# Attention tables on VectorE and ScalarE instead of GpSimd, and the lambda product queued six steps later

## The chip, the core and the metric

The kernel runs on one core of a Trainium2 chip. The metric is the time of one execution on the device in microseconds. The core's engines each work through a queue of their own in order: TensorE (PE, matrix products), VectorE (DVE), ScalarE (ACT), GpSimd (POOL) and SyncE (SP, which here issues the weight loads). An instruction that waits holds up everything behind it on its engine.

## What is computed

Two blocks follow each other on 256 tokens of width 2048 in fp32. The first has dilated-window attention beside bidirectional retention; the second has a layer of differential attention and a layer of forgetting attention. Cut to what the change touches:

```python
# dilated attention: three patterns (window, dilation) share one score matrix
mask = |rel| <= radius and the key lies in the same residue class; bias = -slope * |rel| * dilation
# retention, both directions
decay = where(rel >= 0, exp(max(rel, 0) * log_gamma), 0)
# differential attention: causal mask and ALiBi bias
sc = where(dist >= 0, q @ k - slope * dist, NEG)
lam = exp(sum(lq1 * lk1)) - exp(sum(lq2 * lk2)) + lam_init
a = softmax(sc1) - lam * softmax(sc2)
# forgetting attention: causal mask as an additive NEG
```

Each of these masks and biases is a table that does not depend on the inputs: `dl` (negative distance, hugely negative where no pattern reaches) and `cn` (by how many patterns a key is reached) for the dilated heads, `rp` and `rm` (distance forward and backward, huge on the other side) for retention, `dist` and `tri` for the causal heads. They are made once, when the kernel runs.

## The kernel before, in words

All weights are streamed from HBM in tiles of 128x1024 fp32 (512 KB), each into one of seven `raw` buffers; a buffer is loaded again when its user is done with it. There are two uses. A **projection chunk** is first split for precise fp32 products: ACT casts the tile to `hi` (line 1643), DVE computes `lo` = raw - hi (line 1645), and PE multiplies both parts with the activation tile `hy` (line 145, the helper of all products). There are three buffers of `hi` and of `lo`, and the preparation runs two chunks ahead of PE. A **modulation tile** is multiplied by the conditioning vector and added to an accumulator on DVE alone (line 1623, `acc`). A plan sets how many modulation tiles go between the chunks; up to chunk 13 there is a little more than one to a chunk.

Chunks are counted here from 0. A feature-major chunk is 24 matmuls of 256 columns in eight groups of three (`hi`, `hi`, `lo`), a token-major one twelve of 512. In the first round each projection takes three chunks: 0 to 2 and 3 to 5 are feature-major, 6 to 8 token-major, 9 to 11 feature-major, 12 to 14 token-major. After the last chunk of a projection its four PSUM banks are evacuated by ACT (line 789). There are five such banks, so that the next projection can begin with the fifth.

Small work is written as generators. After each chunk the scheduler's `tick` advances every active generator to its next `yield`, and what they issue goes into the engines' queues at that place. `columns` (begun at chunk 4) transposes loaded vectors with PE, copies them with DVE (lines 489 and 490), makes some constants, and then the elementwise product `lampr` (line 500); PE sums that over the partitions with a product by `ones` (line 503, recorded as line 145), ACT takes the exponential `lame` (line 505), DVE the difference `lam` (line 507). `dilated_tables` runs at the same time, `retention_tables` behind the dilated heads, `causal_tables` behind the retention gates. In all three POOL makes an integer ramp (`iota`) and then does most of the arithmetic, with single operations on DVE: the line 397 for `dl`, the two bitwise ones of line 401. The activation tile of a chunk, where it is not there yet, is made by DVE, ACT, ACT, DVE (lines 642, 633, 635, 636).

Of the kernel before, what the change touches and what calls it, by code (L numbers as in the profile page):

```python
# [9 lines left out]
F32 = mybir.dt.float32  # L10
F32R = mybir.dt.float32r
I32 = mybir.dt.int32
AF = mybir.ActivationFunctionType
ALU = mybir.AluOpType
AX = mybir.AxisListType

P = 128
S = 256
# [3 lines left out]
NEG = -1e30  # L22
HUGE = 1e34
# [75 lines left out]
def two_block_kernel(ctx: ExitStack, tc: tile.TileContext, a: dict, out: bass.AP):  # L99
# [22 lines left out]
    def blk():  # L122
        assert pfree["blk"] > 0
        pfree["blk"] -= 1
        return blkp.tile([P, CW], F32, tag="blk", name=uid("blk"))

    def need_blk(n_):
        return ("wait", lambda: pfree["blk"] >= n_)
# [7 lines left out]
    def t_(shape, tag, bufs=2, dt=F32):  # L136
        return tmp.tile(shape, dt, tag=tag, name=uid(tag), bufs=bufs)

    def c_(shape, name, dt=F32):
        return cst.tile(shape, dt, tag=name, name=name)  # L140

    V, AC, PE, GP = nc.vector, nc.scalar, nc.tensor, nc.gpsimd

    def mm(o, l, r, start, stop):
        PE.matmul(o, l, r, start=start, stop=stop, skip_group_check=True)  # L145
# [131 lines left out]
    make_identity(nc, ident)  # L277
    ones = c_([P, P], "ones")
    GP.memset(ones, 1.0)
    rows = lambda ap: ap.rearrange("o (k p) -> (o k) p", p=P)  # L280
    rows1 = lambda ap: ap.rearrange("(k p) -> k p", p=P)
    xw = a["x"].rearrange("b (t p) d -> p (b t) d", p=P)
# [98 lines left out]
    lg = c_([P, 8], "lg")  # L381

    def dilated_tables():

        for _ in range(4):
            yield ("get", "s")
        yield need_blk(1)
        tab = blk()
        dl, cn = tab[:, 0:512], tab[:, 512:1024]
        iv = t_([P, 512], "s", 4, I32)  # L390
        i2 = t_([P, 512], "s", 4, I32)
        df = t_([P, 512], "s", 4)
        ng = t_([P, 512], "s", 4)
        GP.iota(iv.rearrange("p (a b) -> p a b", a=2), pattern=[[P, 2], [-1, S]], base=S, channel_multiplier=1)
        GP.tensor_copy(df, iv)
        GP.tensor_scalar(df, df, -float(S), None, op0=ALU.add)
        V.scalar_tensor_tensor(dl, df, -1.0, df, op0=ALU.mult, op1=ALU.min)
        GP.tensor_scalar(cn, dl, -64.0, None, op0=ALU.is_ge)
        yield
        for m in (3, 15):  # L400
            V.tensor_scalar(i2, iv, m, None, op0=ALU.bitwise_and)
            GP.tensor_copy(ng, i2)
            GP.tensor_scalar(ng, ng, 0.0, None, op0=ALU.is_equal)
            GP.tensor_tensor(cn, cn, ng, op=ALU.add)
            yield
        GP.tensor_scalar(ng, cn, 0.0, -HUGE, op0=ALU.is_equal, op1=ALU.mult)
        GP.tensor_tensor(dl, dl, ng, op=ALU.add)
        for _ in range(4):
            yield ("free", "s")
        tb["dl"], tb["cn"] = dl, cn  # L410
        ready.add("dl")

    def retention_tables():

        yield from logsig(lg, dec, *(t_([P, 8], "ls", 3) for _ in range(3)))
        V.tensor_scalar(lg, lg, -1e-30, None, op0=ALU.min)
        yield ("get", "s")
        yield ("get", "s")
        yield need_blk(1)
        tab = blk()  # L420
        rp, rm = tab[:, 0:512], tab[:, 512:1024]
        ri = t_([P, 512], "s", 4, I32)
        rf = t_([P, 512], "s", 4)
        GP.iota(ri.rearrange("p (a b) -> p a b", a=2), pattern=[[-P, 2], [1, S]], base=0, channel_multiplier=-1)
        GP.tensor_copy(rf, ri)
        GP.tensor_scalar(rp, rf, 0.0, HUGE, op0=ALU.is_lt, op1=ALU.mult)
        GP.tensor_tensor(rp, rp, rf, op=ALU.add)
        yield
        GP.tensor_scalar(rm, rf, 0.0, HUGE, op0=ALU.is_gt, op1=ALU.mult)
        GP.tensor_tensor(rm, rm, rf, op=ALU.subtract)  # L430
        yield
        yield ("free", "s")
        yield ("free", "s")
        tb["rp"], tb["rm"] = rp, rm
        ready.add("rt")

    def causal_tables():

        yield ("get", "s")
        dist, tri, idr = c_([P, 384], "cz_dist"), c_([P, 256], "cz_tri", F32R), c_([P, P], "cz_id", F32R)  # L440
        ci = t_([P, 384], "s", 4, I32)
        GP.iota(ci[:, 0:256], pattern=[[1, 256]], base=-P, channel_multiplier=-1)
        GP.iota(ci[:, 256:384], pattern=[[1, 128]], base=0, channel_multiplier=-1)
        GP.tensor_copy(dist, ci)
        neg = ci.bitcast(F32)
        GP.tensor_scalar(neg, dist, 0.0, -HUGE, op0=ALU.is_gt, op1=ALU.mult)
        GP.tensor_tensor(dist, dist, neg, op=ALU.add)
        yield
        AC.activation(tri, neg[:, 128:384], AF.Copy, scale=-NEG / HUGE)
        AC.copy(idr, ident)  # L450
        yield
        yield ("free", "s")
        tb["dist"], tb["tri"], tb["idr"] = dist, tri, idr
        ready.add("cz")
# [29 lines left out]
    def columns():  # L484
# [13 lines left out]
        V.tensor_scalar(subc, v3[:, 36:38], 1.0 - LAM_INIT, None, op0=ALU.mult)  # L498
        pr = c_([P, 2], "lampr")
        V.tensor_tensor(pr, v3[:, 32:36:2], v3[:, 33:36:2], op=ALU.mult)  # L500
        pt = yield ("get", "ps")
        mm(pt[:, 0:2], ones, pr, True, True)
        yield
# [1229 lines left out]
```

## Time and profile before

| | us |
|---|---|
| median of 3 runs | 1528.02 (1525.21 to 1530.26) |
| profiled execution | 1529.11 |
| span of the profile, first to last instruction | 1527.3 |
| PE busy | 1482.3 (97%) |
| DVE busy | 1267.4 (83%) |
| ACT busy | 821.7 (54%) |
| POOL busy | 49.5 (3%) |
| HBM read | 433.88 MB, 285 GB/s over the span |

A share of busy time is a mean over stages, so the stretches around the change are read one by one. A timeline row gives the start, the length, the engine and line, the tile written and the tiles read, and in brackets how long the engine idled before it and who ended that. Matmuls overlap, so that a PE row is longer than the distance to the next.

### The profile page before, as it was taken

Reading aid. Unit: us, or ns where it says so; the run is one execution under the profiler, and the core shown is the slowest. Engines: PE = TensorE matmul, PEld = TensorE weight load, DVE = VectorE, ACT = ScalarE, POOL = GpSimd, SP = SyncE. Lnnn points to the kernel's source line nnn. Section 1 sums busy time; section 2 is a strip of 40 time slices with the busy share of each in tenths; the row PEclk is TensorE's granted clock in tenths of the full one; section 3 lists DMA queues with packets and bytes.
Section 4 is the critical chain, followed back from the end, with each engine's and each line's share of the span. In section 5 each row is a group of like instructions: output and inputs, shape, how many; then the busy total and the mean of one; then the engine's idle time right before and its main releaser. Section 6 shows DMA issues by size and latency. Waiting matters only on the chain.

```text
span 1527.3 us, 26803 instructions
## 1 busy us (share of the span) xinstructions
PE 1482.3 (97%) x10152; PEld 1376.9 (90%) x10152; DVE 1267.4 (83%) x1839; ACT 821.7 (54%) x1533; POOL 49.5 (3%) x50
## 2 busy tenths in 40 slices
PE   6899999999999899999999999999999999999997
PEld 5889999989999799899998899978899999999896
DVE  5889989999988787987879989988887856667786
ACT  4474463645644657444555654456444876566631
POOL 3500000021000000000000000000000000000000
PEclk9999999999999999999999999999999999999998
DMA  9899978879699798999788889867999966778761
GB/s 325 291 351 335 351 268 320 314 255 331 212 313 329 249 372 282 356 325 322 254 302 280 293 298 323 272 218 253 312 354 329 328 248 196 245 259 282 258 210 56
DMA packets 180357, 437.75 MB, mean 287 GB/s; under 512 B 16352, under 2 KB 51314, under 8 KB 180228
## 3 DMA queue, kind: packets, MB, share of 16 engines
q1 hardware_dynamic: 179620, 435.89, 82.7%
q8 instruction: 79, 1.29, 0.3%
q14 instruction: 50, 0.41, 0.1%
q0 software_dynamic: 544, 0.14, 0.1%
q10 hardware_dynamic: 64, 0.02, 0.0%
HBM read 433.88 MB, written 2.11 MB: 285 GB/s over the span
## 4 chain that ended last, share of the span: by engine, by line
PE 77%; DVE 12%; DMA 5%; ACT 3%; issue 2%; SPq 0%; DVEq 0%; ACTq 0%
PE pa L145 71%; DVE lo L1645 4%; PE ps L145 4%; DVE acc L1623 3%; DMA w<-fdr 2%; DMA raw<-in_w_ada_dram 2%; ACT hi L1643 2%; PE ps L528 1%; DMA raw<-in_w_in_dram 1%; DMA raw<-in_a_w_in_dram 0%; DVE hy L636 0%; ACT blk L789 0%; ACT w L633 0%; PE ps L1172 0%; DVE xT L657 0%
## 5 line engine op out<-in xcount | busy, mean ns | idle before, releaser
L145 PE MATMUL pa<-hy,hi 128*128 128x256 f32 x4640 | 854.4, 286 | 9.5 <-ACT hy L632 2.7
L1643 ACT CAST hi<-raw 128x1024 fp32r<-128x1024 f32 x463 | 484.5, 1048 | 525.1 <-PE pa L145 443.1
L145 PEld LDWEIGHTS pa<-hy,hi 128*128 128x128 f32 x4640 | 726.4, 192 | 15.1 <-ACT hy L632 3.1
L1645 DVE TENSOR_TENSOR lo<-raw,hi 128x1024 fp32r<-128x1024 f32 x463 | 567.8, 1228 | 201.7 <-ACT hi L1643 200.2
L145 PE MATMUL pa<-hy,lo 128*128 128x256 f32 x2320 | 659.0, 284 | 1.9 <-DVE lo L1645 1.9
L145 PE MATMUL pa<-hi,hy 128*128 128x512 f32 (+1 forms) x1520 | 457.3, 379 | 3.1 <-ACT hy L632 2.3
L145 PEld LDWEIGHTS pa<-hy,lo 128*128 128x128 f32 x2320 | 445.6, 192 | 2.9 <-DVE lo L1645 2.6
L1623 DVE SCALAR_TENSOR_TENSOR acc<-raw,cact,acc 128x1024 f32<-128x1024 f32 (+2 forms) x343 | 423.2, 1237 | 8.9 <-DMA raw<-in_w_ada_dram 8.2
L145 PEld LDWEIGHTS pa<-hi,hy 128*128 128x128 f32 x1520 | 279.0, 189 | 56.7 <-ACT hy L632 3.1
L145 PE MATMUL pa<-lo,hy 128*128 128x512 f32 (+1 forms) x760 | 284.9, 375 | 2.2 <-DVE lo L1645 2.2
L145 PEld LDWEIGHTS pa<-lo,hy 128*128 128x128 f32 x760 | 144.2, 190 | 27.7 <-DVE lo L1645 3.2
L789 ACT ACTIVATE blk<-pa 128x512 f32<-128x512 f32 (+1 forms) x96 | 51.7, 577 | 11.3 <-PE pa L145 8.7
L536 ACT ACTIVATE jk<-ps 128x128 f32<-128x128 f32 x158 | 43.5, 276 | 8.8 <-PE ps L528 5.1
L793 DVE TENSOR_TENSOR blk<-pa,blk 128x512 f32<-128x512 f32 x60 | 37.4, 682 | 0.3 <-PE pa L145 0.3
L145 PE MATMUL ps<-blk,blk 128*128 128x256 f32 (+1 forms) x176 | 37.3, 342 | 0.0
L145 PEld LDWEIGHTS ps<-blk,blk 128*128 128x128 f32 x176 | 30.1, 190 | 3.4 <-DVE blk L793 0.2
L636 DVE TENSOR_TENSOR hy<-w,hy 128x256 fp32r<-128x256 f32 x64 | 27.2, 426 | 5.8 <-ACT w L633 4.9
L536 ACT ACTIVATION_READ_ACCUMULATOR jk<-ps 128x1 f32 x158 | 30.8, 195 | 0.0
L1608 POOL MEMSET acc<- 128x1024 f32 x2 | 1.9, 952 | 859.2 <-PE ps L528 859.2
L633 ACT ACTIVATE w<-xT,B,A 128x256 f32<-128x256 f32 x32 | 19.2, 601 | 11.3 <-DVE xT L663 11.3
L528 PE MATMUL ps<-ident,acc 128*128 128x128 f32 x160 | 24.6, 278 | 0.2 <-DVE acc L1623 0.2
L635 ACT CAST hy<-w 128x256 fp32r<-128x256 f32 x58 | 23.6, 407 | 1.8
(295 smaller groups left out, 818.7 us busy)
## 6 DMA issues: line engine op xcount, KB each, us to landing
raw<-in_w_mod_dram SPq DMA_DIRECT2D x192, 512.0 KB, 5.5
raw<-in_a_w_in_dram SPq DMA_DIRECT2D x128, 512.0 KB, 5.7
raw<-in_w_in_dram SPq DMA_DIRECT2D x112, 512.0 KB, 5.6
raw<-in_w_ada_dram SPq DMA_DIRECT2D x80, 512.0 KB, 5.4
raw<-in_kv_w_mod_dram SPq DMA_DIRECT2D x64, 512.0 KB, 6.2
raw<-in_kv_w_dram SPq DMA_DIRECT2D x64, 512.0 KB, 5.3
raw<-in_b_w_in_dram SPq DMA_DIRECT2D x64, 512.0 KB, 5.1
raw<-in_w_out_dram SPq DMA_DIRECT2D x32, 512.0 KB, 5.2
```

The lines of the kernel that those rows point to most:

```text
L145: PE.matmul(o, l, r, start=start, stop=stop, skip_group_check=True)
L528: PE.transpose(pt[:, j * P : (j + 1) * P], sl.acc[:, (q + j) * P : (q + j + 1) * P], ident)
L536: AC.activation(jk, pt[:, j * P : (j + 1) * P], AF.Copy, accum_out=r[:, q + j : q + j + 1])
L633: AC.activation(hf, t, AF.Identity, bias=bi, scale=sc)
L635: AC.copy(h[:, 0, :], hf)
L636: V.tensor_tensor(h[:, 1, :], hf, h[:, 0, :].bitcast(F32), op=ALU.subtract)
L789: AC.activation(dst, src, AF.Copy, scale=sc)
L793: V.tensor_tensor(dst, src, dst, op=ALU.add)
L1608: GP.memset(sl.acc, 0.0)
L1623: V.scalar_tensor_tensor(ac, tn, c, ac, op0=ALU.mult, op1=ALU.add)
L1643: AC.copy(hi, t)
L1645: V.tensor_tensor(lo, t, hi.bitcast(F32), op=ALU.subtract)
```

## The change

The tables come to the same values in another way. POOL keeps the `iota`s and gets one more constant, `mS`. The steps behind them go to DVE (mostly operations that fuse two steps) and to ACT (conversions from integer, and `Relu(1 - x)` in place of a comparison with zero), one per scheduler step. `rm` now has the other sign, for which `lg[:, 4:8]` is negated. In `columns` six bare `yield`s go between `lampr` and the product that uses it.

```diff
--- before.py
+++ after.py
@@ -277,6 +277,8 @@
     make_identity(nc, ident)
     ones = c_([P, P], "ones")
     GP.memset(ones, 1.0)
+    mS = c_([P, 1], "mS")
+    GP.memset(mS, -float(S))
     rows = lambda ap: ap.rearrange("o (k p) -> (o k) p", p=P)
     rows1 = lambda ap: ap.rearrange("(k p) -> k p", p=P)
     xw = a["x"].rearrange("b (t p) d -> p (b t) d", p=P)
@@ -392,19 +394,26 @@
         df = t_([P, 512], "s", 4)
         ng = t_([P, 512], "s", 4)
         GP.iota(iv.rearrange("p (a b) -> p a b", a=2), pattern=[[P, 2], [-1, S]], base=S, channel_multiplier=1)
-        GP.tensor_copy(df, iv)
-        GP.tensor_scalar(df, df, -float(S), None, op0=ALU.add)
+        yield
+        yield
+        V.tensor_scalar(i2, iv, 3, None, op0=ALU.bitwise_and)
+        yield
+        AC.activation(df, iv, AF.Identity, bias=mS)
+        AC.activation(ng, i2, AF.Relu, bias=ones[:, 0:1], scale=-1.0)
+        yield
         V.scalar_tensor_tensor(dl, df, -1.0, df, op0=ALU.mult, op1=ALU.min)
-        GP.tensor_scalar(cn, dl, -64.0, None, op0=ALU.is_ge)
-        yield
-        for m in (3, 15):
-            V.tensor_scalar(i2, iv, m, None, op0=ALU.bitwise_and)
-            GP.tensor_copy(ng, i2)
-            GP.tensor_scalar(ng, ng, 0.0, None, op0=ALU.is_equal)
-            GP.tensor_tensor(cn, cn, ng, op=ALU.add)
-            yield
-        GP.tensor_scalar(ng, cn, 0.0, -HUGE, op0=ALU.is_equal, op1=ALU.mult)
-        GP.tensor_tensor(dl, dl, ng, op=ALU.add)
+        yield
+        V.scalar_tensor_tensor(cn, dl, -64.0, ng, op0=ALU.is_ge, op1=ALU.add)
+        yield
+        V.tensor_scalar(i2, iv, 15, None, op0=ALU.bitwise_and)
+        yield
+        AC.activation(ng, i2, AF.Relu, bias=ones[:, 0:1], scale=-1.0)
+        yield
+        V.tensor_tensor(cn, cn, ng, op=ALU.add)
+        yield
+        AC.activation(ng, cn, AF.Relu, bias=ones[:, 0:1], scale=-1.0)
+        yield
+        V.scalar_tensor_tensor(dl, ng, -HUGE, dl, op0=ALU.mult, op1=ALU.add)
         for _ in range(4):
             yield ("free", "s")
         tb["dl"], tb["cn"] = dl, cn
@@ -414,6 +423,7 @@
 
         yield from logsig(lg, dec, *(t_([P, 8], "ls", 3) for _ in range(3)))
         V.tensor_scalar(lg, lg, -1e-30, None, op0=ALU.min)
+        V.tensor_scalar(lg[:, 4:8], lg[:, 4:8], -1.0, None, op0=ALU.mult)
         yield ("get", "s")
         yield ("get", "s")
         yield need_blk(1)
@@ -422,12 +432,12 @@
         ri = t_([P, 512], "s", 4, I32)
         rf = t_([P, 512], "s", 4)
         GP.iota(ri.rearrange("p (a b) -> p a b", a=2), pattern=[[-P, 2], [1, S]], base=0, channel_multiplier=-1)
-        GP.tensor_copy(rf, ri)
-        GP.tensor_scalar(rp, rf, 0.0, HUGE, op0=ALU.is_lt, op1=ALU.mult)
-        GP.tensor_tensor(rp, rp, rf, op=ALU.add)
-        yield
-        GP.tensor_scalar(rm, rf, 0.0, HUGE, op0=ALU.is_gt, op1=ALU.mult)
-        GP.tensor_tensor(rm, rm, rf, op=ALU.subtract)
+        yield
+        AC.copy(rf, ri)
+        yield
+        V.scalar_tensor_tensor(rp, rf, -HUGE, rf, op0=ALU.mult, op1=ALU.max)
+        yield
+        V.scalar_tensor_tensor(rm, rf, -HUGE, rf, op0=ALU.mult, op1=ALU.min)
         yield
         yield ("free", "s")
         yield ("free", "s")
@@ -441,13 +451,12 @@
         ci = t_([P, 384], "s", 4, I32)
         GP.iota(ci[:, 0:256], pattern=[[1, 256]], base=-P, channel_multiplier=-1)
         GP.iota(ci[:, 256:384], pattern=[[1, 128]], base=0, channel_multiplier=-1)
-        GP.tensor_copy(dist, ci)
-        neg = ci.bitcast(F32)
-        GP.tensor_scalar(neg, dist, 0.0, -HUGE, op0=ALU.is_gt, op1=ALU.mult)
-        GP.tensor_tensor(dist, dist, neg, op=ALU.add)
-        yield
-        AC.activation(tri, neg[:, 128:384], AF.Copy, scale=-NEG / HUGE)
+        yield
+        AC.copy(dist, ci)
         AC.copy(idr, ident)
+        yield
+        V.tensor_scalar(tri, dist[:, 128:384], NEG, 0.0, op0=ALU.mult, op1=ALU.min)
+        V.scalar_tensor_tensor(dist, dist, -HUGE, dist, op0=ALU.mult, op1=ALU.min)
         yield
         yield ("free", "s")
         tb["dist"], tb["tri"], tb["idr"] = dist, tri, idr
@@ -498,6 +507,8 @@
         V.tensor_scalar(subc, v3[:, 36:38], 1.0 - LAM_INIT, None, op0=ALU.mult)
         pr = c_([P, 2], "lampr")
         V.tensor_tensor(pr, v3[:, 32:36:2], v3[:, 33:36:2], op=ALU.mult)
+        for _ in range(6):
+            yield
         pt = yield ("get", "ps")
         mm(pt[:, 0:2], ones, pr, True, True)
         yield
```

What stands where now is shown at three places. Names are tile names with a buffer number; behind the change a line of the kernel has a number higher by 2 to 11.

PE, at the lambda product (`ps<-lampr,ones`; `hi88` and `lo89` belong to chunk 4, `hi94` and `lo95` to chunk 5). Before:

```order
L145 MATMUL pa100_529<-hy58_347,hi88_473 128x256 x2
L145 MATMUL pa100_529<-hy58_347,lo89_474 128x256
L145 MATMUL ps106_600<-lampr_598,ones_85 128x2
L145 MATMUL pa97_526<-hy83_431,hi94_520 128x256 x2
L145 MATMUL pa97_526<-hy83_431,lo95_521 128x256
```

Now (`hi126` and `lo127` belong to chunk 10, `hi133` and `lo134` to chunk 11):

```order
L145 MATMUL pa139_732<-hy58_349,hi126_686 128x256 x2
L145 MATMUL pa139_732<-hy58_349,lo127_687 128x256
L145 MATMUL ps144_794<-lampr_589,ones_85 128x2
L145 MATMUL pa136_729<-hy83_429,hi133_723 128x256 x2
L145 MATMUL pa136_729<-hy83_429,lo134_724 128x256
```

The product has moved from between chunks 4 and 5 to between chunks 10 and 11; nothing else on PE has moved.

DVE, from chunk 2 to the tables' first operations (`lo68` is chunk 2's, `lo81` chunk 3's, `lo89` chunk 4's, `lo95` chunk 5's, `lo104` chunk 6's; `blk74` holds `dl` and `cn`, `hy83` is an activation tile). Before:

```order
L1645 TENSOR_TENSOR lo68_380<-raw45_308,hi67_379 128x1024
L397 SCALAR_TENSOR_TENSOR blk74_413<-s77_416 128x512
L1623 SCALAR_TENSOR_TENSOR acc51_332<-raw50_330,cact_92,acc51_332 128x1024
L642 TENSOR_TENSOR w182_429<-xT_95,rst_97 128x256
L1645 TENSOR_TENSOR lo81_427<-raw52_334,hi80_426 128x1024
L636 TENSOR_TENSOR hy83_431<-w184_432,hy83_431 128x256
L401 TENSOR_SCALAR s76_415<-s75_414 128x512
...
L1645 TENSOR_TENSOR lo89_474<-raw63_359,hi88_473 128x1024
L401 TENSOR_SCALAR s76_415<-s75_414 128x512
```

Now, from the last of the column constants, which stand behind chunk 6's split as before, to chunk 9 (`lo108` is chunk 7's, `lo115` chunk 8's, `lo123` chunk 9's):

```order
L509 TENSOR_TENSOR lampr_589<-v3_92 128x2
L404 SCALAR_TENSOR_TENSOR blk74_415<-s77_418 128x512
L1634 SCALAR_TENSOR_TENSOR acc51_334<-raw86_462,cact_94,acc51_334 128x1024
L1656 TENSOR_TENSOR lo108_596<-raw87_465,hi107_595 128x1024
L406 SCALAR_TENSOR_TENSOR blk74_415<-blk74_415,s78_419 128x512
L1634 SCALAR_TENSOR_TENSOR acc51_334<-raw90_471,cact_94,acc51_334 128x1024
L1634 SCALAR_TENSOR_TENSOR acc51_334<-raw93_509,cact_94,acc51_334 128x1024
L1656 TENSOR_TENSOR lo115_639<-raw96_515,hi114_638 128x1024
L408 TENSOR_SCALAR s76_417<-s75_416 128x512
L1634 SCALAR_TENSOR_TENSOR acc51_334<-raw102_551,cact_94,acc51_334 128x1024
L1656 TENSOR_TENSOR lo123_665<-raw105_557,hi122_664 128x1024
```

The first table operation has moved from behind chunk 2's split to behind `lampr`; the rest are spread up to chunk 13's split, and one bitwise operation stays behind chunk 4's. `lam`, which stood behind chunk 7's split, now stands behind chunk 13's.

ACT, around the table operations (`hi94` is chunk 5's, `hi103` chunk 6's, `hi133` chunk 11's, `hi141` and `hi145` those of 12 and 13). Now:

```order
L1654 CAST hi94_511<-raw69_385 128x1024
L401 ACTIVATE s77_418<-s75_416,mS_87 128x512
L402 ACTIVATE s78_419<-s76_417,ones_85 128x512
L1654 CAST hi103_553<-raw85_435 128x1024
...
L1654 CAST hi133_723<-raw116_642 128x1024
L414 ACTIVATE s78_419<-blk74_415,ones_85 128x512
L1654 CAST hi141_764<-raw124_668 128x1024
L1654 CAST hi145_797<-raw125_684 128x1024
L800 ACTIVATE blk148_830<-pa136_729 128x512
...
L516 ACTIVATE lame_836<-ps144_794 128x2
```

The activations are new in this queue; `lame` has moved from behind the evacuation of chunks 3 to 5 to behind that of chunks 9 to 11.

## Rows read from the trace of the kernel before

**Rows 1.** the page, part 1: busy us, share of the span, instructions of each engine

```profile
PE 1482.3 (97%) x10152; PEld 1376.9 (90%) x10152; DVE 1267.4 (83%) x1839; ACT 821.7 (54%) x1533; POOL 49.5 (3%) x50
```

**Rows 2.** waits of PE, whole run: us in total, times, longest us

```profile
PE ps L145 <- DVE lampr L500: 4.5, 1, 4.5
```

**Rows 3.** timeline of PE: start, length in us, what, [idle before, releaser]

```profile
45.17 0.38 PE L145 MATMUL pa<-hy,hi 128*128 128x256 f32 x1 [0.52 <-ACT hy L635]
...
59.42 0.56 PE L145 MATMUL ps<-lampr,ones 128*128 128x2 f32 x2 [4.50 <-DVE lampr L500]
59.84 0.77 PE L145 MATMUL pa<-hy,hi 128*128 128x256 f32 x2
...
65.11 0.56 PE L145 MATMUL pa<-hi,hy 128*128 128x512 f32 x1
...
79.21 0.40 PE L145 MATMUL pa<-hy,hi 128*128 128x256 f32 x2
...
82.09 0.40 PE L145 MATMUL pa<-hi,hy 128*128 128x512 f32 x1
```

**Rows 4.** stretch of chunk 5: us, busy us of each engine, granted clock, DMA share, GB/s

```profile
59.40:65.10 5.70, 5.68 (x26) 5.70 (x27) 2.21 (x2) 1.79 (x3) 3.27 (x2) 0.50 0.84 285
```

**Rows 5.** timeline of DVE, 41 to 73 us

```profile
41.77 0.68 DVE L397 SCALAR_TENSOR_TENSOR blk<-s 128x512 f32<-128x512 f32 x1
...
45.79 0.41 DVE L401 TENSOR_SCALAR s<-s 128x512 int32<-128x512 int32 x1
...
50.42 1.55 DVE L401 TENSOR_SCALAR s<-s 128x512 int32<-128x512 int32 x1
...
56.19 2.30 DVE L1645 TENSOR_TENSOR lo<-raw,hi 128x1024 fp32r<-128x1024 f32 x1
...
59.13 0.15 DVE L500 TENSOR_TENSOR lampr<-v 128x2 f32<-128x2 f32 x1
...
66.04 0.16 DVE L507 TENSOR_TENSOR lam<-lame 128x1 f32<-128x1 f32 x1 [4.43 <-ACT lame L505]
...
71.15 1.22 DVE L1645 TENSOR_TENSOR lo<-raw,hi 128x1024 fp32r<-128x1024 f32 x1
72.29 1.28 DVE L1623 SCALAR_TENSOR_TENSOR acc<-raw,cact,acc 128x1024 f32<-128x1024 f32 x1
```

**Rows 6.** timeline of POOL, the last operation but one of the dilated tables

```profile
57.50 2.79 POOL L406 TENSOR_SCALAR s<-blk 128x512 f32<-128x512 f32 x1
```

**Rows 7.** stretches: columns as in Rows 4 (PE, PEld, DVE, ACT, POOL)

```profile
25.00:50.00 25.00, 18.68 (x104) 16.75 (x105) 21.31 (x31) 12.73 (x29) 7.37 (x3) 1.00 1.01 372
50.00:70.00 20.00, 15.50 (x89) 14.50 (x88) 15.49 (x21) 7.12 (x10) 11.90 (x7) 0.83 0.71 244
...
75.00:110.00 35.00, 34.60 (x221) 30.95 (x219) 30.01 (x45) 24.28 (x50) 0.00 (x0) 1.00 1.01 352
110.00:140.00 30.00, 29.21 (x240) 28.74 (x239) 29.00 (x36) 14.88 (x20) 0.00 (x0) 1.00 0.91 325
```

**Rows 8.** timeline of ACT, three casts of chunks

```profile
75.85 1.05 ACT L1643 CAST hi<-raw 128x1024 fp32r<-128x1024 f32 x1 [1.59 <-DMA raw<-in_w_in_dram]
...
143.47 1.06 ACT L1643 CAST hi<-raw 128x1024 fp32r<-128x1024 f32 x1 [2.85 <-DMA raw<-in_w_in_dram]
...
165.53 1.05 ACT L1643 CAST hi<-raw 128x1024 fp32r<-128x1024 f32 x1 [1.83 <-PE pa L145]
```

**Rows 9.** chain of waits back from 130 us: start, length, what

```profile
31.93 7.33 DMA raw<-in_w_ada_dram
```

**Rows 10.** the page, part 5: busy us, mean ns of one, idle before

```profile
L789 ACT ACTIVATE blk<-pa 128x512 f32<-128x512 f32 (+1 forms) x96 | 51.7, 577 | 11.3 <-PE pa L145 8.7
```

**Rows 11.** timeline of DVE, a split beside the retention tables

```profile
327.93 2.31 DVE L1645 TENSOR_TENSOR lo<-raw,hi 128x1024 fp32r<-128x1024 f32 x1
```

**Rows 12.** timeline of PE behind that split

```profile
330.30 0.50 PE L145 MATMUL pa<-lo,hy 128*128 128x512 f32 x1 [0.56 <-DVE lo L1645]
```

**Rows 13.** stretch of the causal tables, columns as in Rows 7

```profile
370.00:385.00 15.00, 15.00 (x79) 13.01 (x78) 14.66 (x16) 9.12 (x22) 5.76 (x5) 1.00 0.71 240
```

## The prediction, made before the changed kernel was run

> **What bounds the kernel now.** I read the page first, then the list of waits, then the stretches in which something waits. TensorE (PE) is busy for 97% of the span [rows 1], so a microsecond counts only where PE stands still or runs at a lower clock. The longest single wait of PE after its start is 4.5 us, for the product that gives lambda (`lampr`) [rows 2].
>
> The timeline of PE shows the place [rows 3]. PE idles 4.50 us, the product begins at 59.42, chunk 5 at 59.84. Chunk 5 then runs at half the rate: its 24 matmuls take 59.84 to 65.11 = 5.27 us, where the like ones of chunk 11 take 79.21 to 82.09 = 2.88. The granted clock was 0.50 in that stretch [rows 4], which is 1.2 of 2.4 GHz, after 4.5 us in which PE had idled.
>
> Why `lampr` is late is in the timeline of VectorE (DVE) [rows 5]: it comes at 59.13, behind the split of chunk 6 (`lo`, 56.19), which takes 2.30 us where 1.22 is usual (71.15). The bitwise table operation at 50.42 takes 1.55, the same one 0.41 at 45.79. These two alone cost 2.2 us. GpSimd (POOL) works on the tables beside them, 2.79 us for one operation [rows 6]. DVE afterwards idles 4.43 us more for `lam` [rows 5], which needs an exponential on ScalarE (ACT) that stands behind the evacuation of chunk 5.
>
> A stalled DVE frees no raw buffers, so transfers stop: 372 GB/s in 25 to 50, 244 in 50 to 70, then 352 in 75 to 110 [rows 7]. The loads are close behind PE here: ACT waits for a transfer at 75.85 and still at 143.47; at 165.53 it waits for PE [rows 8]. So what PE gains before 80 us must be fed by transfers up to some 145, and is then kept to the end, since the order of every engine is unchanged beyond the tables and lambda.
>
> **The change, part by part.** The sum is made against the profiled execution, 1529.1 us, which is 1.1 above the median of 1528.0.
>
> *Lambda product six steps later.* It goes from behind chunk 4 to behind chunk 10. Its operand is made behind the split of chunk 6, so at chunk 10 it has long been there: -4.5 us. The product's own 0.42 (59.42 to 59.84) moves along; I count nothing for it. With no idling ahead of it chunk 5 runs like chunk 11: 2.88 - 5.27 = -2.4 us.
>
> *POOL's eleven operations on the dilated tables.* Chunk 2 waits 0.52 us for its activation tile (45.17) [rows 3]. Ahead of that tile in DVE's order stands the first table operation (41.77, 0.68) [rows 5], which now comes some four chunks later. Between 0 and -0.5; I take -0.5, since more than that leaves the queue. PE's demand is thus 7.4 us earlier from chunk 6 on.
>
> *Six operations on DVE instead of three.* DVE's operations follow each other about 0.08 sooner than their length (71.15 + 1.22 against 72.29) [rows 5]. Two bitwise ones at 0.33 and four of 0.60 come to 3.1 us, against 1.3 for the three of before without stretching. Is DVE in time? From 39.3, when the tile of an accumulation has just landed (31.93 + 7.33) [rows 9], to the split of chunk 11 the new order has 13 accumulations at 1.19 (15.5, from 72.29), ten splits at 1.14 (11.4), five table operations (2.5), the column constants (0.8, from the end of 56.19 to that of 59.13) and two operations of 256 elements for one activation tile (0.7, an estimate from the 0.68 of 512): 30.9 us, so 70.2 without a wait. PE began chunk 11 at 79.21 and will want it at 71.8. It fits by 1.6: cost 0, as long as the transfers keep up.
>
> *Do they?* Behind the tile of 39.3 up to chunk 11's own 21 must land: twelve for accumulations, nine for chunks 3 to 11, of 524,288 bytes, 11.0 MB. At 372 GB/s that is 29.6 us, so 68.9; with 1.05 for the cast `hi` [rows 8] and 1.22 for `lo` the chunk is ready at 71.2, in time. At the 352 of 75 to 110 it is 31.3 us, ready at 72.9, 1.1 late. At the 325 of 110 to 140 it is 33.8 us and 3.6 late [rows 7]. So this step gives back between 0 and 3.6; I take +1.1, since 75 to 110 is the nearest stretch in which the loads were catching up.
>
> *ACT.* Four activations of 128x512 at about 0.58 [rows 10] are put between its casts: two behind the cast of chunk 5, one behind that of chunk 9, one behind that of chunk 11. Their operands come from DVE operations that stand ahead of those casts' splits, so I expect no waiting. The cast of chunk 6 comes up to 1.2 us later; its split ends by 55.7 (58.5 now, less 2.2 and 0.6), and PE wants it at 57.7. Cost 0; wholly uncovered, the four would be 2.3. The two later tables add three small copies or casts to an engine busy for 54% [rows 1], less one activation: 0.
>
> The Trainium skill's page "ScalarE: Activation LUTs", section "Rules for kernel authors", speaks against this part: relu, max, add and the like belong on VectorE, not on ScalarE. By its figures (section "What ACT_TABLE_LOAD costs": 280 ns and 0.833 ns an element with a pointer bias) an activation of 512 would take 0.71 us, an estimate. The row's 0.58 is lower, and decides. By the page the sum would lose up to 2.8 us, if nothing covered the four.
>
> *Retention tables, 308 to 330.* POOL's chain stretches DVE here too: the split at 327.93 takes 2.31 us instead of 1.22 [rows 11], and PE waits 0.56 for it at 330.30 [rows 12]. That 1.1 goes, and two operations of 0.60 and a tiny one come to DVE, one of them behind this split: -0.5 (0 to -0.56).
>
> *Causal tables, near 375.* DVE gets two operations. PE is busy for all of 370 to 385 [rows 13] and has two chunks ready ahead of it: 0. POOL's new memset of one column, 0.1 us ahead of its first DMAs, delays nothing that PE waits for: 0.
>
> Sum: -4.5 - 2.4 - 0.5 + 1.1 - 0.5 = **-6.8 us**. The profiled execution would take 1522.3, the median 1521.2.
>
> **The rivals.**
> - *The loads do not follow.* The hole of 50 to 70 is not filled, since raw buffers still come free too slowly with DVE full for 30.9 of 32.5 us. With the 244 GB/s of before [rows 7] chunk 11 would be ready at 86.7, later than now: no gain is left. Between that and the 3.6 of the part above lie 1524 to 1528, say 1525.5. Against it: 25 to 50 ran at 372 with DVE busy for 21.3 of 25 us. Chance 0.17.
> - *All of it* (faster still). The transfers run at 372 and nothing is given back: -4.5 - 2.4 - 0.5 - 0.56 = -8.0, and up to 1 us more where loads came late behind the hole (the wait at 75.85): 1519.5 or less. Against it: DVE itself then has 1.6 us to spare and no more. Chance 0.14.
> - *ACT's detour costs* (the rule above as a mechanism). The casts of chunks 6, 10 and 12 come up to 2.3 us late in all and nothing covers it: -4.5, so 1523.5. For it: splits and matmuls meet closely under the new demand. Against: ACT idles 1.83 us before a cast when all is in time (165.53). Chance 0.05.
> - *The wait returns as `lam` on DVE* (slower). `lam` now stands behind the split of chunk 13, and its exponential on ACT behind the evacuation of chunks 9 to 11, thus behind PE. If DVE gets there two chunks ahead of PE, it waits 5.8 us and four evacuations, 2.4: 8.2. Nothing frees a buffer meanwhile, and a new transfer takes 7.3 to land [rows 9]; PE has the two chunks, 5.8, so it idles 9.7 and then runs at half the clock for some two chunks, 4.8. Less the 7.9 gained that is +6.6: 1534.6. From a wait of 6.3 us on it is slower by 0.3%. Against: by the counts above DVE is not before 74.5 at `lam`, and PE ends chunk 11 at 74.7, with some 0.8 of evacuation and exponential behind it: a wait of about 1 us. Chance 0.05.
> - *The product waits again* (no change). That needs `lampr` to come later than chunk 10 in DVE's time, while it stands behind the split of chunk 6, four chunks earlier. Chance 0.01.
>
> **How the numbers follow.** The forecast has the remaining 0.58. About 0.3% (4.6 us) is what a measurement of this kernel can tell from no change, so faster means below 1523.4. The forecast, but for its edge where 3.6 is given back, and the larger gain lie there, with a little of the ACT case: 0.73. Same: the loads' case, that edge, the rest of ACT's: 0.22. Slower: 0.05. The range of 1517 to 1526 takes in the larger gain, with the scatter of the runs below it, and most of the loads' case.
>
> **What would show it.** Right: no PE wait on `lampr`; granted clock 1.00 from 45 to 90; splits of 1.2 us in 45 to 62; chunk 11 beginning near 72; 350 GB/s or more in 50 to 70; POOL with little but iotas and memsets; no wait at 330. Wrong: PE waits for `lo`, or ACT for transfers, for more than 3 us together in 60 to 90, or DVE waits for `lam` over 4 us again.

## The result, and the profile after

The changed kernel takes 1518.14 us (median, 1517.29 to 1520.17), the kernel before 1527.74 in the same session: ratio 0.9935, 95% interval 0.9917 to 0.9953, that is 9.6 us less. It was measured once more, in another session, at 1520.62 against 1527.63: ratio 0.9955, 0.9940 to 0.9971, 7.0 us less. The profiled execution took 1518.92 us, with a span of 1517.1. Two of the executions timed below ran far longer than the rest, one of the later product alone (5111.66 us) and one of POOL's work without its use (1678.05); the ratios leave them out, and without them the two medians would be 1525.14 and 1527.11.

The page, part 1, of the changed kernel [rows 1]:

```profile
PE 1479.0 (97%) x10152; PEld 1375.5 (91%) x10152; DVE 1262.9 (83%) x1847; ACT 824.3 (54%) x1538; POOL 13.2 (1%) x32
```

The shares of PE, DVE and ACT are those of before; POOL alone shows the change. The waits say more. Waits of PE in the changed kernel, whole run (us in total, times, longest), the first, the fifth and the sixth:

```profile
PE ps L299 <- DMA s<-in_c_dram: 5.5, 1, 5.5
...
PE pa L145 <- ACT blk L800: 3.4, 1, 3.4
PE pa L145 <- DVE lo L1656: 2.7, 3, 1.6
```

The row for `lampr` [rows 2] is gone, and in 38 to 100 us, where before had waits of 4.5, 0.5 and 0.4 us, this view is empty. The timeline of PE shows the same places as [rows 3]:

```profile
44.49 0.66 PE L145 MATMUL pa<-hy,hi 128*128 128x256 f32 x2
...
53.59 0.40 PE L145 MATMUL pa<-hy,hi 128*128 128x256 f32 x2
...
56.47 0.40 PE L145 MATMUL pa<-hi,hy 128*128 128x512 f32 x1
...
70.41 0.28 PE L145 MATMUL ps<-lampr,ones 128*128 128x2 f32 x2
70.54 0.48 PE L145 MATMUL pa<-hy,hi 128*128 128x256 f32 x2
70.86 0.28 PE L145 MATMUL pa<-hy,lo 128*128 128x256 f32 x1
```

Chunk 2 begins at 44.49 without a wait. Chunk 5 runs from 53.59 to 56.47 = 2.88 us instead of 5.27. The lambda product at 70.41 waits for nothing and is 0.13 ahead of chunk 11 at 70.54 (79.21 before, 71.8 forecast). Stretches of the changed kernel, columns as in [rows 7]:

```profile
25.00:50.00 25.00, 19.54 (x113) 17.96 (x113) 21.39 (x30) 13.67 (x31) 0.00 (x0) 1.00 1.02 372
50.00:70.00 20.00, 20.00 (x137) 18.57 (x136) 19.93 (x26) 12.36 (x18) 0.00 (x0) 1.00 1.04 392
```

In 50 to 70 us the clock is 1.00 where it was 0.83, PE and DVE are busy throughout, and the loads move 392 GB/s where they moved 244. The timeline of DVE shows why [rows 5, 11]:

```profile
44.28 0.43 DVE L647 TENSOR_TENSOR hy<-w,hy 128x256 fp32r<-128x256 f32 x1
...
52.14 1.22 DVE L1656 TENSOR_TENSOR lo<-raw,hi 128x1024 fp32r<-128x1024 f32 x1
...
53.97 0.15 DVE L509 TENSOR_TENSOR lampr<-v 128x2 f32<-128x2 f32 x1
54.05 0.68 DVE L404 SCALAR_TENSOR_TENSOR blk<-s 128x512 f32<-128x512 f32 x1
...
69.34 1.22 DVE L1656 TENSOR_TENSOR lo<-raw,hi 128x1024 fp32r<-128x1024 f32 x1
70.48 1.28 DVE L1634 SCALAR_TENSOR_TENSOR acc<-raw,cact,acc 128x1024 f32<-128x1024 f32 x1
...
74.57 0.16 DVE L518 TENSOR_TENSOR lam<-lame 128x1 f32<-128x1 f32 x1
...
320.63 1.22 DVE L1656 TENSOR_TENSOR lo<-raw,hi 128x1024 fp32r<-128x1024 f32 x1
```

Chunk 6's split (52.14) and those of the retention stage (320.63) take 1.22 us again, `lampr` comes at 53.97 instead of 59.13, and `lam` (74.57) has no wait. Chunk 11's split ends at 70.56; PE begins that chunk at 70.54 and first reads `lo` at 70.86. DVE's last operation on the activation tile of chunk 2 (44.28) takes 0.43 us; before, with POOL at work, it took 0.72:

```profile
45.15 0.72 DVE L636 TENSOR_TENSOR hy<-w,hy 128x256 fp32r<-128x256 f32 x1
```

On ACT, two of the new activations and two casts behind them:

```profile
49.31 0.73 ACT L401 ACTIVATE s<-s,mS 128x512 f32<-128x512 int32 x1
49.93 0.71 ACT L402 ACTIVATE s<-s,ones 128x512 f32<-128x512 int32 x1
...
60.90 1.06 ACT L1654 CAST hi<-raw 128x1024 fp32r<-128x1024 f32 x1 [1.56 <-DMA raw<-in_w_in_dram]
...
70.10 1.05 ACT L1654 CAST hi<-raw 128x1024 fp32r<-128x1024 f32 x1 [0.92 <-DMA raw<-in_w_in_dram]
```

The activations take 0.71 to 0.73 us, and ACT still has time to wait for transfers.

**Where the time came from.** PE's order is the same but for the lambda product, so the start of a matmul can be compared with that of the same one before. The table gives, for every profile taken, how much earlier (-) or later PE is than in the first profile of before: at transposes near 31, 52, 290 and 345 us, at the last transposes of `acc` near 1064, at the chunk that waits for `blk` near 1296, and at the end of the span (times of before, us).

| kernel | 31 | 52 | 290 | 345 | 1064 | 1296 | end |
|---|---|---|---|---|---|---|---|
| after | -0.3 | -1.2 | -8.7 | -9.6 | -7.2 | -7.8 | -10.2 |
| after_again | +0.5 | -0.4 | -7.8 | -8.7 | -7.4 | -7.2 | -3.6 |
| before_again | -0.1 | -0.1 | -0.7 | -0.7 | +1.8 | +2.4 | +2.5 |
| one_step | -0.1 | -1.0 | -8.8 | -9.7 | -8.3 | -8.0 | -8.4 |
| tables_only | +0.3 | -0.6 | -6.3 | -7.1 | -5.6 | -6.0 | -1.7 |
| dil_only | -0.9 | -1.8 | -8.9 | -8.8 | -8.8 | -7.5 | -5.5 |
| dve_all | +1.5 | +0.6 | -6.3 | -7.1 | -6.3 | -6.6 | -7.2 |
| warm_first | +0.1 | +0.5 | -7.4 | -8.2 | -7.3 | -7.5 | -7.9 |
| lam_only | +0.3 | +0.3 | -3.1 | -3.1 | -2.4 | -2.8 | -5.8 |
| fill_wait | +0.7 | +0.7 | -2.2 | -2.2 | +0.6 | +1.9 | +4.3 |
| pool_beside | +0.7 | +0.2 | +0.1 | -0.8 | -0.6 | -1.1 | -0.4 |

Less the difference at the start, the change has gained 9.3 us by 345 us (9.2 in after_again). Nothing of it lies in the code behind that; what the columns do there is a matter of its own, below.

### The profile page after: what moved, and what is told of

Its sections match the earlier page's. It is cut to its first block, busy times and chain, and to the rows that moved or that the text cites. A ratio compares the mean times of both kernels' runs of the same rounds, so it can differ in the third digit from the quotient of the medians.

```text
span 1517.1 us, 26792 instructions
## 1 busy us (share of the span) xinstructions
PE 1479.0 (97%) x10152; PEld 1375.5 (91%) x10152; DVE 1262.9 (83%) x1847; ACT 824.3 (54%) x1538; POOL 13.2 (1%) x32
## 4 chain that ended last, share of the span: by engine, by line
PE 82%; DVE 9%; DMA 3%; ACT 3%; issue 2%; SPq 0%; DVEq 0%; ACTq 0%
PE pa L145 76%; PE ps L145 4%; DVE lo L1656 3%; DMA w<-fdr 2%; DVE acc L1634 2%; ACT hi L1654 1%; PE ps L539 1%; DMA raw<-in_w_ada_dram 1%; DMA raw<-in_x_dram 1%; DVE hy L647 0%; PE ps L1183 0%; DVE xT L668 0%; ACT blk L800 0%; PE ps L969 0%; ACT w L644 0%
## 5 line engine op out<-in xcount | busy, mean ns | idle before, releaser
L644 ACT ACTIVATE w<-w,B,A 128x256 f32<-128x256 f32 x32 | 19.2, 601 | 8.3 <-DVE w L653 4.8
```

The source lines that it names most:

```text
L644: AC.activation(hf, t, AF.Identity, bias=bi, scale=sc)
```

## The experiments

All ratios are to the kernel before, timed on the same chip, with 95% intervals; its median was 1528.43 us beside the first four, 1528.34 beside the next four and 1527.63 beside the last two.

### The later product alone

The kernel before with the six steps, POOL's chains as they were:

```diff
         V.tensor_tensor(pr, v3[:, 32:36:2], v3[:, 33:36:2], op=ALU.mult)
+        for _ in range(6):
+            yield
         pt = yield ("get", "ps")
```

> The kernel before with the six steps ahead of the lambda product alone; the tables stay on GpSimd. Theory (the 4.5 us wait is a matter of where the product stands in PE's queue, and GpSimd's stretching of VectorE is only what made its operand late): the wait on lampr and the half clock of chunk 5 go, -6.9 us, but VectorE is still stretched, so PE waits some 0.5 to 1.5 us in all for the splits of chunks 6 and 7, and the retention tables' wait of 0.56 stays: 5.5 to 6.5 us under the kernel before, about 1522. Rival (the stretching is the cause and the wait only its sign): PE waits for the split of chunk 6 in place of lampr, 3 us or more, and runs at half clock again: at most 3 us gained, 1525.

1525.68 us, ratio 0.9985 (0.9969 to 1.0002). In the trace PE is 3.4 us ahead at 290 us, less the start. Waits of PE in 38 to 100 us, and the stretch of 50 to 70:

```profile
PE pa L145 <- DVE lo L1647: 2.2, 2, 1.7
PE pa L145 <- ACT blk L791: 0.8, 1, 0.8
PE pa L145 <- DVE hy L638: 0.4, 1, 0.4
```

```profile
50.00:70.00 20.00, 17.67 (x110) 15.21 (x109) 19.96 (x21) 10.48 (x14) 12.24 (x7) 1.00 0.84 285
```

The wait for `lampr` is gone and the clock stays at 1.00, which should give 4.5 + 2.4 = 6.9. But 3.0 us of new waits stand in their place, since the splits are as late as before and now the next chunks meet them, and the loads move only 285 GB/s. So the result lies between theory and rival: half of the gain needs no faster DVE, half does.

### The tables alone

The changed kernel without the six steps:

```diff
         V.tensor_tensor(pr, v3[:, 32:36:2], v3[:, 33:36:2], op=ALU.mult)
-        for _ in range(6):
-            yield
         pt = yield ("get", "ps")
```

> The changed kernel without the six steps: the product stands behind chunk 4 again. Theory: without GpSimd beside it VectorE makes lampr at 54.1 as in the changed kernel, PE is through with chunk 4 at 53.2 and waits 0.9 to 1.2 us, too little to halve its clock: about 1.5 us slower than the changed kernel, 1519.5. Rival (the place in the queue is the cause): the wait stays at 3 us or more with half the clock behind it, 1524 or more.

1518.57 us (1516.38 to 1527.40), ratio 0.9951 (0.9929 to 0.9972). Waits of PE in 38 to 100 us:

```profile
PE pa L145 <- ACT hy L644: 0.7, 1, 0.7
PE ps L145 <- DVE lampr L509: 0.5, 1, 0.5
PE pa L145 <- DVE lo L1654: 0.4, 1, 0.4
```

Without POOL's work the product waits 0.5 us at its old place instead of 4.5. At 345 us PE is 7.4 us ahead, less the start, against 9.3 with the steps. So nearly four fifths of the gain come from the tables alone; the steps add up to 1.9 us in the traces, which the medians cannot tell from nothing.

### PE kept busy through the wait

The kernel before with nine products ahead of lambda's, into the same bank; nothing reads what they write, and lambda's product writes its own two columns anew:

```diff
         pt = yield ("get", "ps")
+        for _ in range(9):
+            mm(pt[:, 0:S], ident, xT[:, 0, :], True, True)
         mm(pt[:, 0:2], ones, pr, True, True)
```

> The kernel before with nine products of 256 columns, whose results are not used, ahead of the lambda product, so that PE works through most of the wait. Theory (chunk 5 runs at half rate because PE had idled): granted clock 1.00 behind the product, chunk 5 takes 2.9 us instead of 5.3, and the time falls by 2.4 us less what the nine products take beyond the wait (0 to 0.5): 1525.5 to 1526. Rival (chunk 5 is slow for another reason, its data or VectorE): chunk 5 takes 5.3 us again, no gain or a small loss.

1529.64 us, ratio 1.0008 (0.9991 to 1.0026). The stretch of 50 to 70 us and the wait that is left:

```profile
50.00:70.00 20.00, 19.46 (x122) 17.48 (x121) 18.12 (x22) 8.92 (x14) 12.63 (x7) 1.00 0.85 282
```

```profile
PE ps L145 <- DVE lampr L500: 0.5, 1, 0.5
```

`lampr` is as late as before, but PE does not idle and the clock stays at 1.00. Chunk 5 takes 2.94 us (60.29 to 63.23 in PE's timeline) instead of 5.27, and PE is 2.9 us ahead at 290 us, less the start: the clock's part of the loss is a term of its own, 2.3 us against the 2.4 of the forecast. The time of this kernel does not show it, since the profiled execution lost 6.5 us between 345 us and its end, where profiles differ for another reason (the last two runs).

### The dilated tables and lambda alone

The changed kernel with the retention and causal tables of before (their code restored word for word; cut here):

```diff
-        AC.copy(rf, ri)
-        yield
-        V.scalar_tensor_tensor(rp, rf, -HUGE, rf, op0=ALU.mult, op1=ALU.max)
-        yield
-        V.scalar_tensor_tensor(rm, rf, -HUGE, rf, op0=ALU.mult, op1=ALU.min)
+        GP.tensor_copy(rf, ri)
+        GP.tensor_scalar(rp, rf, 0.0, HUGE, op0=ALU.is_lt, op1=ALU.mult)
+        GP.tensor_tensor(rp, rp, rf, op=ALU.add)
+        yield
+        GP.tensor_scalar(rm, rf, 0.0, HUGE, op0=ALU.is_gt, op1=ALU.mult)
+        GP.tensor_tensor(rm, rm, rf, op=ALU.subtract)
...
```

> The changed kernel with the retention tables made as before on GpSimd; dilated and causal tables and the lambda product as changed. Theory: the wait of PE near 320 for a stretched split is back with 0.5 to 0.6 us, and the place of the retention transposes is 0.6 to 1.0 us later; the stretch up to 300 is as in the changed kernel: 1518.8 to 1519.2. Rival (that table is hidden): no difference from the changed kernel at that place.

1524.05 us, ratio 0.9968 (0.9948 to 0.9987). The split beside POOL and the only wait of PE in 300 to 400 us:

```profile
319.12 2.31 DVE L1656 TENSOR_TENSOR lo<-raw,hi 128x1024 fp32r<-128x1024 f32 x1
```

```profile
PE pa L145 <- DVE lo L1656: 0.7, 1, 0.7
```

From 290 to 345 us PE gains nothing here (-8.9, -8.8), and 0.8 to 0.9 in each of the seven profiles with the new tables. That is the worth of the later tables. The median lies further from the changed kernel's than this 0.9; no row ties the rest to those tables, and the profiled execution lost 3.3 us behind 345 us. It stays open.

### POOL's work without its use

The tables as in the kernel of the tables alone, and beside them nine operations of POOL of the kinds and sizes that were taken out, on a tile of their own (one small DVE operation starts them in time):

```diff
         GP.iota(iv.rearrange("p (a b) -> p a b", a=2), pattern=[[P, 2], [-1, S]], base=S, channel_multiplier=1)
+        pb_ = c_([P, 512], "poolb")
+        GP.memset(pb_, -1.0)
+        V.tensor_scalar(pb_[:, 0:1], ones[:, 0:1], -1.0, None, op0=ALU.mult)
+        GP.tensor_scalar(pb_, pb_, -64.0, None, op0=ALU.is_ge)
+        for m in (3, 15):
+            GP.tensor_copy(pb_, iv)
+            GP.tensor_scalar(pb_, pb_, 0.0, None, op0=ALU.is_equal)
+            GP.tensor_tensor(pb_, pb_, pb_, op=ALU.add)
+        GP.tensor_scalar(pb_, pb_, 0.0, -1.0, op0=ALU.is_equal, op1=ALU.mult)
+        GP.tensor_tensor(pb_, pb_, pb_, op=ALU.add)
```

> The changed kernel without the six steps, and with a chain of nine GpSimd operations of 128x512 on a tile of their own beside VectorE, begun where the kernel before began its chain; their results are not used. Theory (GpSimd reading SBUF stretches VectorE's two-input operations): splits and bitwise operations in 42 to 62 take up to 2.3 us again, lampr comes 2 to 4 us later than the 54.1 of the changed kernel, PE waits 3 to 4.5 us for it and runs chunk 5 at half the clock: 4 to 7 us slower than the same kernel without the chain. Rival (the gain came from the operations leaving VectorE's own order): VectorE as in the changed kernel, under 1 us.

1527.33 us, ratio 0.9990 (0.9974 to 1.0006). The longest wait of PE in 38 to 100 us, a stretch, and DVE's timeline:

```profile
PE ps L145 <- DVE lampr L519: 3.6, 1, 3.6
```

```profile
60.00:70.00 10.00, 10.00 (x46) 9.00 (x46) 6.10 (x9) 4.44 (x7) 2.38 (x1) 0.75 0.56 191
```

```profile
54.12 1.63 DVE L1642 SCALAR_TENSOR_TENSOR acc<-raw,cact,acc 128x1024 f32<-128x1024 f32 x1
55.67 2.09 DVE L1664 TENSOR_TENSOR lo<-raw,hi 128x1024 fp32r<-128x1024 f32 x1
...
58.40 0.15 DVE L519 TENSOR_TENSOR lampr<-v 128x2 f32<-128x2 f32 x1
...
68.70 1.22 DVE L1664 TENSOR_TENSOR lo<-raw,hi 128x1024 fp32r<-128x1024 f32 x1
```

Nobody waits for these nine operations, and yet everything is back: a split of 2.09 us while POOL works, 1.22 behind it (68.70), `lampr` at 58.40, a wait of 3.6, half the clock in chunk 5 (0.50 in 58.20 to 65.00), 191 GB/s. Not every operation beside POOL is longer: a split at 60.27 took 1.21, and there it was POOL's own last operation that took 2.75 us, where two like it had taken 1.33 and 1.04. Of the gain at 290 us 0.6 is left, less the start, against 6.5 without POOL's work. So it was not that DVE or ACT waited for POOL's results. POOL stretched DVE's operations by working beside them. The Trainium skill's page "SBUF — State Buffer", section "Who interferes with whom", has a rule for this: a DVE instruction with two SBUF inputs contends with a GpSimd instruction that reads SBUF. The splits here have two inputs, and agree: 2.09 us beside POOL's work, 1.22 behind it.

### One step instead of six

The changed kernel with one bare step behind `lampr`:

```diff
-        for _ in range(6):
-            yield
+        yield
         pt = yield ("get", "ps")
```

> The changed kernel with one step ahead of the lambda product instead of six: it stands behind chunk 5. Theory: lampr is there at 54.1 and PE ends chunk 5 at 56.4, so no wait, and VectorE reaches lam behind the split of chunk 8 or so and waits under 1 us: same as the changed kernel within 0.5 us in the profile. Rival (lam in VectorE's queue costs): VectorE idles 2 us or more for lam, transfers fall under 300 GB/s and PE waits for splits.

1519.25 us (1515.39 to 1520.63), ratio 0.9927 (0.9905 to 0.9949), and 9.6 us ahead at 345 us, less the start: the same as with six. No wait for `lampr` is left. One chunk of distance is enough once `lampr` comes in time.

### ACT's activations on DVE

The four activations of the dilated tables as DVE operations:

```diff
-        AC.activation(df, iv, AF.Identity, bias=mS)
-        AC.activation(ng, i2, AF.Relu, bias=ones[:, 0:1], scale=-1.0)
+        V.tensor_scalar(df, iv, -float(S), None, op0=ALU.add)
+        V.tensor_scalar(ng, i2, 0.0, None, op0=ALU.is_equal)
...
-        AC.activation(ng, i2, AF.Relu, bias=ones[:, 0:1], scale=-1.0)
+        V.tensor_scalar(ng, i2, 0.0, None, op0=ALU.is_equal)
...
-        AC.activation(ng, cn, AF.Relu, bias=ones[:, 0:1], scale=-1.0)
+        V.tensor_scalar(ng, cn, 0.0, None, op0=ALU.is_equal)
```

> The changed kernel with the four activations of the dilated tables made by VectorE operations instead, as the rule for relu and add has it. Theory (VectorE and the transfers are the tight ones here): VectorE gets 1.3 to 2 us more up to chunk 13 and PE waits 0.5 to 1.5 us in all for splits of chunks 9 to 13: 1519 to 1519.7. Rival (by the rule): ScalarE is freed by 2.9 us, no wait on PE, same time or up to 0.5 us less.

1521.98 us, ratio 0.9951 (0.9934 to 0.9967). Such an operation is shorter on DVE, 0.42 us against 0.72, but DVE is the fuller engine. PE's timeline has one wait more, in chunk 11, of the kind that the forecast feared for the change itself:

```profile
73.34 0.39 PE L145 MATMUL pa<-hy,lo 128*128 128x256 f32 x1 [0.56 <-DVE lo L1656]
```

At 345 us PE is 8.6 us ahead, less the start, against 9.2 and 9.3; the intervals of the times overlap. So the shorter operation brings no gain here. In 50 to 70 us of the changed kernel DVE is busy for 19.93 of 20 us, ACT for 12.36.

### A faster start

In the changed kernel, as in before, the first chunks run slowly. From one pair of matmuls to the next it takes 0.64 us at 36.92 and 0.36 at 42.33 (PE's timeline). The profile of the changed kernel holds no record of the clock before 41.9 us, so the 1.00 that its view gives for 36.6 to 41.5 says nothing. The profile of the kernel with one step has one, and on its PE the pairs are 0.64 us apart up to 40.26 and 0.36 from 40.83:

```profile
36.60:40.20 3.60, 3.60 (x17) 3.60 (x18) 3.57 (x4) 1.98 (x3) 0.00 (x0) 0.50 1.03 385
```

The granted clock is 0.50 there and 1.00 in 41.00 to 44.40, so the slow start is half the clock. Three unused products ahead of chunk 0, to keep PE busy through its waits there:

```diff
+    warm(3)
     sched.add(dilated_tables())
```

> The changed kernel with three products of 256 columns, whose results are not used, between the transposes of the first modulation slice and chunk 0, where PE idles 2.7 us. Theory (an idle PE runs at half rate behind it): chunk 0 takes 2.9 us instead of 4.9, -2 us, of which the loads may take back up to 1: 1516.5 to 1517. Rival (three products are too few, or the activation tile of chunk 1 and 2 is the next limit): chunk 0 as before, or PE waits for the tile of chunk 2 instead: same time.

1520.98 us, ratio 0.9952 (0.9935 to 0.9969), no faster. PE's timeline, in chunk 0 and at chunk 2:

```profile
37.01 0.40 PE L145 MATMUL pa<-hy,hi 128*128 128x256 f32 x2
37.37 0.40 PE L145 MATMUL pa<-hy,hi 128*128 128x256 f32 x2
...
44.64 1.04 PE L145 MATMUL pa<-hy,hi 128*128 128x256 f32 x2 [2.08 <-ACT hy L646]
```

Chunk 0 runs at 0.36 a pair from the start, but PE then stands 2.08 us at chunk 2, whose activation tile is not ready, and behind that wait the clock is low again:

```profile
44.60:48.20 3.60, 3.55 (x15) 3.29 (x16) 3.55 (x4) 1.98 (x5) 0.00 (x0) 0.53 1.04 403
```

What PE wins ahead of DVE and ACT it waits for later, and then pays for the wait: at 345 us it is 8.3 us ahead, less the start, against 9.3 in the changed kernel.

### Both kernels once more

Unaltered, to see how much two profiles of one kernel differ.

> The changed kernel unaltered, profiled a second time and timed beside the variants' own reference. Theory: the change itself is worth 8.5 to 9.6 us, all of it before 340 us, and what the two traces differ by later is scatter of the clock behind the short stops of PE between stages. Then at 290 us and at 333 us PE is again 8 to 9.5 and 9 to 10 us ahead of the first trace of before, less what it starts earlier or later (under 1.5), while the difference behind 480 us is another one than in the first trace, by up to 2 us either way at single stages. The median is 1518 to 1520. Rival: the late differences belong to the change; then the losses near 500 and 1000 us (1.4 and 0.9) and the gain of 1.8 in the last 20 us are found again with the same signs and sizes.

> The kernel before unaltered, a second profile. Theory: it waits for lampr again, 4 to 5 us, chunk 5 runs at half the clock, the split in the retention stage again takes over 2 us, so that up to 340 us it lies within 1.5 us of the first trace of before; behind 480 us it wanders from it by 1 to 3 us without any change to the kernel. Rival: the two traces of the same kernel agree within 0.5 us at every stage, so that a late difference between two kernels has a cause in their code.

After_again 1520.62 us (1518.19 to 1525.45), ratio 0.9955 (0.9940 to 0.9971); before_again 1529.06 (1526.89 to 1533.71), ratio 1.0010 (0.9998 to 1.0022). Before_again waits for `lampr` as before; waits of PE, whole run:

```profile
PE ps L145 <- DVE lampr L500: 4.5, 1, 4.5
```

At the table's places up to 345 us the two profiles of before agree within 0.7 us and those of the changed kernel within 0.9; less the start, no matmul up to there differs by more than 0.7 in either pair. At the end they are 2.5 and 6.6 us apart. Two places hold 3.5 of these 6.6. One is a wait of PE for the evacuation of a projection, the other the last products. Of the changed kernel, first profile: PE's timeline, and the stretch:

```profile
1350.70 0.51 PE L145 MATMUL pa<-hy,hi 128*128 128x256 f32 x2 [3.38 <-ACT blk L800]
...
1352.96 0.60 PE L1376 MATMUL ps<-ident,xT 128*128 128x128 f32 x4
...
1511.11 1.98 PE L145 MATMUL pa<-blk,s 2*128 2x512 f32 x4 [0.34 <-ACT s L1464]
```

```profile
1340.00:1360.00 20.00, 16.62 (x137) 16.31 (x136) 12.18 (x13) 12.68 (x25) 0.00 (x0) 1.00 0.78 253
```

The second profile of the same kernel, the same views:

```profile
1352.92 0.80 PE L145 MATMUL pa<-hy,hi 128*128 128x256 f32 x2 [3.40 <-ACT blk L800]
...
1356.93 1.06 PE L1376 MATMUL ps<-ident,xT 128*128 128x128 f32 x4
...
1515.90 3.77 PE L145 MATMUL pa<-blk,s 2*128 2x512 f32 x4 [0.34 <-ACT s L1464]
```

```profile
1340.00:1360.00 20.00, 16.60 (x114) 16.10 (x113) 12.32 (x12) 12.77 (x27) 0.00 (x0) 0.83 0.77 242
```

Behind the same wait, 3.38 and 3.40 us, the clock stays at 1.00 in one execution and falls in the other; the work up to the transposes takes 2.26 and 4.01 us. The same four last products take 1.98 and 3.77, behind the same wait of 0.34. Before has both forms too, in PE's timeline of its first and its second profile:

```profile
1519.55 3.77 PE L145 MATMUL pa<-blk,s 2*128 2x512 f32 x4 [0.34 <-ACT s L1453]
```

```profile
1523.82 1.98 PE L145 MATMUL pa<-blk,s 2*128 2x512 f32 x4 [0.34 <-ACT s L1453]
```

So the late differences are not the change's, as the theory has it. The rival is out: the gain of 1.8 in the last 20 us is absent in the second profile of the changed kernel and present in the second of before. One thing of it holds: near 500 us both profiles of the changed kernel lose (1.4 and 0.9), but before_again loses 0.5 there itself against the first profile of before.

## Why the prediction was right

The forecast was 1521.2 us, from -6.8. Both medians, 1518.14 and 1520.62, lie in the range and on the side that had the chance of 0.73. The first lies in the rival "all of it"; that rival's own sum, -8.0, gives 1520.0, so that its 1519.5 needs part of the extra 1 us it names. By the traces this rival held, with 9.3 us gained and nothing given back: the mechanism of the forecast was right, its sum 2.5 us short. Step by step, against PE's times up to 345 us:

- **The wait for `lampr`, -4.5:** right; it is gone in the changed kernel, and the tables alone cut it to 0.5.
- **Chunk 5 at full clock, -2.4:** right; 2.88 us was forecast and measured. The clock's part was isolated by the kernel that only fills the wait (2.94 us for the chunk).
- **The product itself, "I count nothing for it":** 0.42 became 0.13 at the full clock, a gain of 0.3 that was left out.
- **Chunk 2, -0.5:** mis-sized; PE gains 0.9 between 31 and 52 us in after, after_again, one_step, tables_only, dil_only and dve_all. The forecast priced one wait of PE, 0.52 at 45.17. What counts is when the activation tile is ready: at 45.87 before (45.15 + 0.72) and at 44.71 now (44.28 + 0.43), 0.9 earlier less the start. Some 0.6 of that is the table operation ahead of it (0.68, less the 0.08 by which operations overlap), as forecast; 0.3 is the tile's own last operation, which POOL no longer stretches. In pool_beside that operation takes 0.72 again, and PE gains only 0.5 by 52 us.
- **Extra work on DVE, 0:** right, with 0.3 us to spare instead of 1.6: chunk 11's split ends at 70.56, near the 70.2 of the forecast, but PE came earlier than forecast and first reads it at 70.86. Moving four more operations to DVE brought 0.56 us of wait back at just this chunk.
- **The loads' give-back, +1.1:** wrong. The failed step is "I take +1.1, since 75 to 110 is the nearest stretch". With DVE busy for 19.93 of 20 us the loads ran at 392 GB/s in 50 to 70, above the 372 of the range's better end; after_again had 366, one_step 373. From 52 to 290 us PE lost nothing: it went from 7.4 ahead near 85 to 7.6 (less the 1.2 of 52 us).
- **ACT, 0:** right in sum, with the price wrong. The activations take 0.71 to 0.73 us, not 0.58; the row taken was that of an evacuation, the nearest by size but with other inputs, and its mean mixes two shapes (0.595 for 128x512 alone). Casts near them still wait 0.9 to 1.6 us for transfers, which is the cover. The Trainium skill's page "ScalarE: Activation LUTs", section "What ACT_TABLE_LOAD costs", gave an estimate of 0.71, and that was the right figure. The rule in the Trainium skill's page "ScalarE: Activation LUTs", section "Rules for kernel authors", that such operations belong on VectorE, is not borne out here, as dve_all is no faster.
- **Retention tables, -0.5:** mis-sized; -0.8 to -0.9 in seven profiles. The wait row says 0.56, but PE's matmuls show more: from 329.26 to the one that waits until 330.30 it is 1.04 us, where the next such pair, 333.31 to 333.62, is 0.31 apart. That is 0.73 of it.
- **Causal tables, 0:** right; from 345 to 394 us nothing changes.

With these sizes the sum is -4.5 - 2.4 - 0.3 - 0.9 + 0 - 0.85 = -8.95 against the 9.3 measured. The 0.3 left over was not traced.

The forecast allowed 0.3%, 4.6 us, for what a measurement of this kernel can tell. The two medians of one kernel, 9.6 and 7.0 us under before, differ by 2.6, more than any single term turned out to be off, so that the times alone cannot say which step was mis-sized. The traces up to 345 us were the better measure, as that part repeats within 0.7 us, less the start.

## What to carry to other kernels

- When an engine off the critical path works beside a busy one, look for operations of the busy engine that are longer there than elsewhere. To learn whether the cause is waiting or contention, keep the work and take away its use, as pool_beside does.
- Moving a late consumer back only moves the wait to the next consumer, as in lam_only; making the producer in time was worth about twice as much.
- Where a change acts in an early stage, compare the start of the same instruction in both traces just behind that stage, and profile both kernels twice, before explaining a difference at the end.

## What was not expected of the hardware

- After equal waits in the same program, the granted clock went either way: 1.00 and 0.83 (means over 20 us; 0.50 in 1352.00 to 1357.00 of the second) behind 3.38 and 3.40 us, and 1.98 or 3.77 us for the last four products (0.50 in 1515.80 to 1520.00 of the slower one). Each such place is worth about 1.8 us, and which way it goes differs between executions of one kernel.
- Work of POOL that nobody waits for is dear: nine operations, 19 us of POOL, cost PE 5.9 us by 290 us (pool_beside against tables_only, less the start). The time agrees: 0.9990 against 0.9951 of before is 6.0 us. The medians are 8.8 apart, with runs of tables_only from 1516.38 to 1527.40.
- In 50 to 70 us the loads moved 244 GB/s in both profiles of before, and 337 (tables_only) to 392 (after) in the seven without POOL's work there. Two profiles of the changed kernel had 392 and 366, so that the highest figure is not one to count on.
